# Output projections by Strassen's scheme, sums made ahead, and layer 1's values projected token by token

## The chip, the core and the metric

The kernel runs on one core of a Trainium2 chip. The metric is the device time of one execution in microseconds (us). Names of engines: PE is TensorE's matmuls, PEld its weight loads, DVE is VectorE, ACT is ScalarE, POOL is GpSimd, SP is SyncE, whose queue issues nearly all DMAs here.

## What is computed

Two layers over 1024 tokens of width 1024, all in float32. A layer normalises x, projects it, runs several groups of attention heads, multiplies their outputs with a gate, and projects the result y (1536 columns) back to 1024 columns, which are added to x:

```python
# layer 0                                   # layer 1
ya = global_gqa(qa, ka, va)                 yc = neighborhood_attn(qc, kc, vc, rpb_c[o])
yb = window_gqa(qb, kb, vb, sink, bias)     ym = memory_attn(qm, mk, mv)
ym = memory_attn(qm, mk, mv)                y = concatenate([yc, ym]) * silu(gate)
y = concatenate([ya, yb, ym]) * silu(gate)  x = x + y @ w_out_odd[o]
x = x + y @ w_out_even[e]                   return rmsnorm(x, final_norm_gain)
```

The product `y @ w_out` (1024 x 1536 times 1536 x 1024) is the output projection, once in each layer. Layer 1's neighbourhood attention has 16 heads of 64, which the kernel takes in 8 pairs, each with its own queries, keys and values projected from the normalised x.

## The kernel before

Everything is held transposed: 128 channels on the partitions, tokens along the row. Each float32 matrix is split into two parts, h (rounded) and l (the rest), and a product is three matmuls: h·h, h·l and l·h. So a projection of 128 channels over 512 tokens from 1024 inputs is 8 x 3 = 24 matmuls of 128x512. A weight unit is 4 blocks of 128x128: one DMA to `wraw` (`wload`, L100), then `wparts` (L112) makes `wh` and `wl` (L120 on POOL; L121 on DVE in layer 0 and on POOL in layer 1). There are four buffers of each.

The stages are: "prep" (memory keys, first projections), "l0" (four global head pairs with four memory heads between, then four window pairs), the output projection of layer 0, "l1" (four memory heads, then eight neighbourhood pairs, `near_head` L855), and the output projection of layer 1. A head's chain goes over all engines: scores on PE, row maximum on DVE, exponential on ACT, reciprocal on DVE, scaling on POOL (L815, L905), transposes on PE (`flip`, L96), split of the transposed tile on ACT and DVE (`p_parts`, L357), and the product with v on PE. Projections of the next heads stand between these steps on PE (`tokens`, L145, matmuls at L192), so that PE has work while a chain runs on. The order on each engine is not written by hand: the framework's list scheduler sets it when the kernel is built, from priorities (`AHEAD`, `ahead`) and its own idea of durations. Each engine then keeps to its order, and waits for semaphores.

The gated output of a head pair goes to DRAM (`gated`, L340, into `yd`) and is read back by the output projection (`y_parts`, L916). In layer 1 each pair's v is projected channel by channel (`v_pair`, L305) and then turned to tokens on the partitions by four transposes for each half (`v_sink`, L310, flips at L98).

`out_project` (L933) runs over two halves of 512 tokens, in each over 8 blocks of 128 output channels, and for each block over 12 blocks of y: 8 x 12 x 3 = 288 matmuls of 128x512 for a half, 576 for a layer (L136; the last block of all in two quarters of 256 tokens, L1001). After a block it adds x (L956), squares the sum (L957) and adds up the squares (L967); `done` then makes the norm of the half from them.

## Time and profile before

| | |
|---|---|
| median of 3 runs | 1590.55 us (1590.38 to 1591.15) |
| the profiled execution | 1589.67 us, of it 1587.5 us from the first to the last instruction (the span) |
| PE busy | 1541.1 us, 97% of the span, 8392 matmuls |
| DVE, ACT, POOL busy | 60%, 45%, 39% of the span |
| mean granted TensorE clock | 0.988 of full speed |
| moved by DMA | 167.46 MB, 105 GB/s over the span |

A busy share is an average over stages that differ. Matmuls are pipelined: one that lasts 0.4 us follows the one before it after less, so PE's pace is read from the starts. Idle time counts where something waits for the engine.

### The profile page before, as it was taken

The page shows a single profiled execution, that of the slowest core. Times are in us where ns is not written, and L with a number is a line of the kernel's source. Part 1 is how long each engine was busy: PE and PEld are TensorE (multiplying, and loading weights), DVE is VectorE, ACT ScalarE, POOL GpSimd, SP SyncE. Part 2 cuts the span into 40 slices and gives each one's busy share as a digit, 9 for nine tenths or more (in the row PEclk, how much of TensorE's full clock was granted, in tenths as well). Part 3 has the DMA queues.
Part 4 walks back from the last instruction along what each step waited for, and adds up shares of the span by engine and source line. Part 5 has one row for each costly group of instructions (what it writes and reads, how often), then busy time and mean ns, then how long its engine had stood idle before and what let it go on. Part 6 is the DMA issues. An engine that isn't in the chain of part 4 may idle for free.

```text
span 1587.5 us, 24171 instructions
## 1 busy us (share of the span) xinstructions
PE 1541.1 (97%) x8392; PEld 1322.0 (83%) x8392; DVE 952.8 (60%) x2123; ACT 707.1 (45%) x1626; POOL 626.7 (39%) x753
## 2 busy tenths in 40 slices
PE   6999999999999999989999999999999999999997
PEld 5899888988888788868778888888888888887886
DVE  7768677768776668855743444555556555554122
ACT  7644565566655445632213343444544444543110
POOL 2522324323322223325453344433433443445884
PEclk7999999999999999999999999999999999999998
DMA  9535211021101211146452232213223222235672
GB/s 352 178 100 160 83 34 55 20 87 47 60 14 54 89 41 57 57 147 209 153 177 81 87 112 88 77 69 102 73 73 102 71 75 89 83 108 186 228 261 80
DMA packets 96633, 167.46 MB, mean 105 GB/s; under 512 B 9472, under 2 KB 28160, under 8 KB 96512
## 3 DMA queue, kind: packets, MB, share of 16 engines
q1 hardware_dynamic: 95648, 165.19, 31.6%
q8 instruction: 66, 1.08, 0.3%
q10 hardware_dynamic: 864, 0.74, 0.2%
q14 instruction: 55, 0.45, 0.1%
HBM read 121.85 MB, written 34.60 MB: 99 GB/s over the span
## 4 chain that ended last, share of the span: by engine, by line
PE 89%; DVE 4%; DMA 3%; ACT 2%; issue 1%; POOL 0%; DVEq 0%; SPq 0%; ACTq 0%; POOLq 0%
PE pj L192 42%; PE tr L98 8%; PE sa L136 8%; PE pj L136 6%; PE pv L838 4%; PE s L136 3%; PE pj L637 3%; PE pv L874 2%; PE sa L807 2%; PE sa L808 2%; PE s L891 1%; PE s L892 1%; PE pv L535 1%; DMA wraw<-w_mem 1%; PE pj L390 1%
## 5 line engine op out<-in xcount | busy, mean ns | idle before, releaser
L192 PE MATMUL pj<-H,wh 128*128 128x512 f32 x1952 | 634.5, 402 | 2.2 <-ACT bt L957 1.5
L192 PEld LDWEIGHTS pj<-H,wh 128*128 128x128 f32 x1952 | 351.2, 188 | 64.8 <-POOL wh L120 1.9
L192 PE MATMUL pj<-H,wl 128*128 128x512 f32 x976 | 386.3, 396 | 0.0
L120 POOL TENSOR_SCALAR wh<-wraw 128x512 fp32r<-128x512 f32 x226 | 151.2, 671 | 433.4 <-PE pj L192 281.8
L90 ACT ACTIVATE ph<-tr 128x512 fp32r<-128x512 f32 (+2 forms) x336 | 178.4, 540 | 218.3 <-PE tr L98 204.9
L363 DVE TENSOR_TENSOR pl<-tr,ph 128x512 fp32r<-128x512 f32 (+2 forms) x336 | 205.2, 616 | 81.8 <-ACT ph L90 78.3
L192 PEld LDWEIGHTS pj<-H,wl 128*128 128x128 f32 x976 | 183.6, 188 | 38.1
L121 POOL TENSOR_TENSOR wl<-wraw,wh 128x512 fp32r<-128x512 f32 x136 | 178.9, 1321 | 24.6 <-ACT wh L90 14.5
L815 POOL TENSOR_SCALAR P<-P,st 128x1024 f32<-128x1024 f32 x64 | 80.3, 1256 | 128.2 <-DVE st L814 126.9
L905 POOL TENSOR_SCALAR pn<-pn,st 128x384 f32<-128x384 f32 (+1 forms) x128 | 71.2, 564 | 145.0 <-DVE st L904 144.0
L121 DVE TENSOR_TENSOR wl<-wraw,wh 128x512 fp32r<-128x512 f32 x116 | 91.7, 801 | 59.7 <-POOL wh L120 45.3
L98 PE MATMUL tr<-ident,P 128*128 128x128 f32 x816 | 122.5, 273 | 0.6 <-DVE pl L363 0.6
L98 PEld LDWEIGHTS tr<-ident,P 128*128 128x128 f32 x816 | 96.4, 140 | 9.8 <-DVE pl L363 2.3
L903 ACT ACTIVATE pn<-pn,st 128x384 f32<-128x384 f32 (+1 forms) x128 | 74.4, 582 | 46.7 <-DVE st L902 45.8
L813 ACT ACTIVATE P<-sa,st 128x1024 f32<-128x1024 f32 x64 | 71.5, 1117 | 40.4 <-PE tr L98 19.8
L812 DVE TENSOR_REDUCE st<-sa 128x1 f32<-128x1024 f32 x64 | 77.5, 1216 | 8.2 <-PE sa L808 8.1
L267 DVE TENSOR_TENSOR vt<-pj,rows 128x512 f32<-128x512 f32 x60 | 41.4, 689 | 67.5 <-PE pj L192 67.5
L899 DVE CUSTOM_DVE_ANT_0 pn<-s,bm 128x384 f32<-128x384 f32 x96 | 51.3, 554 | 44.6 <-PE s L892 40.8
L637 PE MATMUL pj<-ah,H 128*128 128x256 f32 x384 | 72.5, 285 | 0.0
L90 ACT ACTIVATE bt<-pv 64x512 f32<-64x512 f32 (+1 forms) x80 | 40.8, 510 | 60.5 <-PE pv L874 24.7
L838 PE MATMUL pv<-ph,va 128*128 128x256 f32 x256 | 66.7, 285 | 0.0
L838 PE MATMUL pv<-pl,va 128*128 128x256 f32 x256 | 65.4, 281 | 0.0
(324 smaller groups left out, 3096.4 us busy)
## 6 DMA issues: line engine op xcount, KB each, us to landing
wraw<-w_o SPq DMA_DIRECT2D x80, 256.0 KB, 2.6
wraw<-w_oe SPq DMA_DIRECT2D x48, 256.0 KB, 2.8
wraw<-w_oo SPq DMA_DIRECT2D x48, 256.0 KB, 2.9
wraw<-w_e SPq DMA_DIRECT2D x44, 256.0 KB, 2.6
k<-k SPq DMA_DIRECT2D x36, 256.0 KB, 3.7
wraw<-w_mem SPq DMA_DIRECT2D x32, 256.0 KB, 4.0
y<-yb SPq DMA_DIRECT2D x12, 512.0 KB, 2.6
y<-sg SPq DMA_DIRECT2D x24, 256.0 KB, 2.4
```

Source lines behind the costliest of these rows:

```text
L90: return self.nc.scalar.activation(out, in_, AF.Copy, scale=scale)
L98: self.turned = self.fence = self.nc.tensor.transpose(o, i, self.ident)
L120: nc.gpsimd.tensor_scalar(hf, raw, 1.0, 1.0, op0=OP.mult, op1=OP.mult)
L121: (nc.gpsimd if self.wsplit[1] == "pool" else nc.vector).tensor_tensor(lf, raw, hf, op=OP.subtract)
L136: self.last = nc.tensor.matmul(a[:, :n], s[:, k, :], moving(u * UNIT + k, c, n)[m], start=(u == units[0] and k == 0 and i == 0), stop=(u = ...
L192: last = nc.tensor.matmul(a[:, :n], s[:, kt % UNIT, :], m, start=(kt == 0 and i == 0), stop=(kt == KT - 1 and i == 2))
L363: nc.vector.tensor_tensor(pl[:, :n], tr[:, :n], ph[:, :n], op=OP.subtract)
L637: self.last = nc.tensor.matmul(a[:, b * 256:(b + 1) * 256], x[kt][:, t], w, start=(kt + b + i == 0), stop=(kt == KT - 1 and i == 2), skip_ ...
L812: nc.vector.tensor_reduce(st[:, 0:1], s, axis=AX.X, op=OP.max, negate=True)
L815: nc.gpsimd.tensor_scalar(pt, pt, st[:, 2:3], 0.5, op0=OP.mult, op1=OP.mult)
L838: nc.tensor.matmul(o[:, :256], v[:, c + k, kv, :], part[:, k * 256:(k + 1) * 256], start=(c + k == 0 and part is parts[0]), stop=(c + k == ...
L903: nc.scalar.activation(o, o, AF.Exp, bias=st[:, 1:2], accum_out=st[:, 2:3])
```

## The change

Both output projections are computed by Strassen's scheme in Winograd's form. The 1024 output channels, the 1536 y channels and the 1024 tokens are each cut in two, and the product of two 2x2 block matrices is made by 7 block products in place of 8. A block product is 4 blocks of 128 channels x 6 blocks of y x 3 matmuls of 128x512. The four sums of weight blocks (`weight_sums`) are made on POOL during layer 0's global heads and on DVE during layer 1's `values`, in pieces of 128x192, and go to DRAM (`sd`). The sums of y are made by POOL when a head's output is gated (`gated`) and go to DRAM in `yd`; the pairs are paired by `ROWS`, so that six head outputs come first and the other six each read their partner's sums back. `y_parts` loads one block of y for each product and splits it on ACT and DVE. The products' results are added into x on DVE as they come (`plus`). Weights of the output projections now come in units of 3 blocks, split on ACT and, in turn, DVE and POOL (`w_parts`).

Layer 1's values are no longer made pair by pair: `values` makes four pairs' v at once, with tokens on the partitions straight away (x as the stationary operand), in 8 blocks of 128 tokens x 24 matmuls, twice, between the memory heads; v goes to DRAM (`vd`), and each neighbourhood pair loads its own. In "l0" the l part of every weight unit moves from DVE to POOL.

```diff
-            with self.phase("l0", ("pool", "dve"), ...
+            with self.phase("l0", ("pool", "pool"), ...

+    def values(self, w, vd, g, side):
...
+        for b in range(8):
+            next(side, None)
+            p = self.ps("pj")
+            t = slice(b * 128, b * 128 + 128)
+            for kt, (h, l) in enumerate(ws):
+                for i, (x, m) in enumerate(((self.h[0], h), (self.h[0], l), (self.h[1], h))):
+                    nc.tensor.matmul(p, x[kt][:, t], m, start=(kt + i == 0), stop=(kt == KT - 1 and i == 2))
...
     def gated(self, sg, y, dst, other=None):
+            nc.vector.tensor_tensor(y, y, sg, op=OP.mult)
+            if other is None:
+                nc.gpsimd.tensor_tensor(sg[:, first], y[:, first], y[:, second], op=OP.subtract)
...
+            else:
+                nc.sync.dma_start(dst[:, 0:2, :], two(y))
+                nc.sync.dma_start(two(sg), other[:, 0:2, :])
+                nc.gpsimd.tensor_tensor(sg[:, second], y[:, first], sg[:, second], op=OP.subtract)
+                nc.gpsimd.tensor_tensor(sg[:, first], y[:, first], sg[:, first], op=OP.subtract)
+                nc.sync.dma_start(dst[:, 2:4, :], two(sg))
+                nc.gpsimd.tensor_tensor(y[:, second], sg[:, second], y[:, second], op=OP.subtract)
+                nc.sync.dma_start(dst[:, 4, :], y[:, second])
...
+        def sums():                                   # in weight_sums, 16 units of 4 sums
+            engine.tensor_tensor(a22, a22, a21, op=OP.add)
+            engine.tensor_tensor(a21, a11, a21, op=OP.subtract)
+            engine.tensor_tensor(a11, a22, a11, op=OP.subtract)
+            engine.tensor_tensor(a12, a12, a11, op=OP.subtract)
...
+        def product(y, bank, ws, start, cols=slice(0, 512)):
+            for u, (h, l) in enumerate(ws):
+                for k in range(3):
+                    for e, (s, m) in enumerate(((h, 0), (h, 1), (l, 0))):
+                        last = nc.tensor.matmul(bank, s[:, k, :], y[3 * u + k][m][:, cols], ...
...
+        for i in range(4):
+            product(first, xb[i], weights(i, "a11"), True)
...
+            product(y, yb[i], weights(i, "s1"), True)
+            product(y, xb[i], weights(i, "s2"), False)
+            product(y, xb[i], weights(i, "s3"), False)
+            product(y, yb[i], weights(i, "s4"), False)
...
+                end = product(y, xb[i], parts, True)          # a12
+            product(y, xb[i], weights(i, "a22"), True)
```

In layer 0's global heads the sums stand between the scalings of the softmax on POOL. Before, for the first head pair (P are the softmax tiles, st their statistics):

```order
L815 TENSOR_SCALAR P_2328<-P_2328,st_2327 128x1024
L120 TENSOR_SCALAR wh_2867<-wraw_2865 128x512
L815 TENSOR_SCALAR P_2375<-P_2375,st_2374 128x1024
L815 TENSOR_SCALAR P_2418<-P_2418,st_2417 128x1024
L815 TENSOR_SCALAR P_2469<-P_2469,st_2468 128x1024
```

And the same stretch of POOL now:

```order
L870 TENSOR_SCALAR P_2343<-P_2343,st_2342 128x1024
L1025 TENSOR_TENSOR bias_2289<-bias_2289 128x192
L129 TENSOR_SCALAR wh_2909<-wraw_2907 128x512
L870 TENSOR_SCALAR P_2396<-P_2396,st_2395 128x1024
L1026 TENSOR_TENSOR bias_2289<-bias_2289 128x192
L130 TENSOR_TENSOR wl_2910<-wraw_2907,wh_2909 128x512
L1027 TENSOR_TENSOR bias_2289<-bias_2289 128x192
L870 TENSOR_SCALAR P_2439<-P_2439,st_2438 128x1024
L1028 TENSOR_TENSOR bias_2289<-bias_2289 128x192
L870 TENSOR_SCALAR P_2493<-P_2493,st_2492 128x1024
```

Four sums and the l part of a weight unit came in; at most two added instructions stand in front of a scaling.

At the end of layer 0's last window pair, PE before (L535 is the product with v, L136 the output projection, k, q tiles of y, sa and pv banks of PSUM):

```order
L535 MATMUL pv_7715<-ph_7763,v_6090 128x2x128
L535 MATMUL pv_7715<-pl_7764,v_6090 128x2x128
L535 MATMUL pv_7715<-ph_7774,v_6090 128x2x128
L535 MATMUL pv_7715<-pl_7775,v_6090 128x2x128
L136 MATMUL sa_7915<-k_7875,wh_7991 128x512 x2
L136 MATMUL sa_7915<-k_7875,wl_7992 128x512
```

And PE now (L590 is the product with v, L1082 `product`):

```order
L1082 MATMUL tr_8087<-k_8230,wh_8267 128x512 x2
L1082 MATMUL tr_8087<-k_8230,wl_8268 128x512
L590 MATMUL pv_7925<-pl_7974,v_6278 128x2x128
L590 MATMUL pv_7925<-ph_7984,v_6278 128x2x128
L590 MATMUL pv_7925<-pl_7985,v_6278 128x2x128
L1082 MATMUL sa_8085<-q_8227,wh_8316 128x512 x2
L1082 MATMUL sa_8085<-q_8227,wl_8317 128x512
```

Here q_8227 and k_8230 hold sums of y that don't need the last pair. The first matmul that needs the last pair's y comes after 99 others of 128x512 (at the end of layer 1, after 93).

At the end of the program DVE made the first quarter's output (tr_16491) before the second quarter's norm (rq_v_16554 to iq_y_16556):

```order
L1118 SCALAR_TENSOR_TENSOR bm_16216<-bm_16216,gain_65,tr_16491 128x256 x2
L239 TENSOR_SCALAR rq_v_16554<-pv_16549 128x2
L1118 SCALAR_TENSOR_TENSOR yb_16339<-yb_16339,gain_65,tr_16491 128x256 x2
L1118 SCALAR_TENSOR_TENSOR yb_16408<-yb_16408,gain_65,tr_16491 128x256 x2
L571 RECIPROCAL iq_y_16556<-iq_t_16557 128x2
L572 TENSOR_TENSOR iq_t_16557<-iq_y_16556 128x2
L573 SCALAR_TENSOR_TENSOR iq_t_16557<-iq_t_16557,rq_v_16554 128x2
L574 SCALAR_TENSOR_TENSOR iq_y_16556<-iq_t_16557,iq_y_16556 128x2
L1118 SCALAR_TENSOR_TENSOR bm_16216<-bm_16216,gain_65,tr_16563 128x256 x2
```

Now both norms come first, and both outputs after them:

```order
L626 RECIPROCAL iq_y_16933<-iq_t_16934 128x2
L628 SCALAR_TENSOR_TENSOR iq_t_16880<-iq_t_16880,rq_v_16877 128x2
L627 TENSOR_TENSOR iq_t_16934<-iq_y_16933 128x2
L629 SCALAR_TENSOR_TENSOR iq_y_16879<-iq_t_16880,iq_y_16879 128x2
L628 SCALAR_TENSOR_TENSOR iq_t_16934<-iq_t_16934,rq_v_16931 128x2
L629 SCALAR_TENSOR_TENSOR iq_y_16933<-iq_t_16934,iq_y_16933 128x2
L1303 SCALAR_TENSOR_TENSOR H_15748<-H_15748,gain_65,tr_16886 128x256 x2
L1303 SCALAR_TENSOR_TENSOR yb_15753<-yb_15753,gain_65,tr_16886 128x256 x2
L1303 SCALAR_TENSOR_TENSOR yb_15754<-yb_15754,gain_65,tr_16886 128x256 x2
L1303 SCALAR_TENSOR_TENSOR H_15748<-H_15748,gain_65,tr_16940 128x256 x2
```

All twelve output instructions now stand behind the last norm.

## Rows read from the trace of the kernel before

**Rows 1.** The chain that ended last: shares of the span by engine.

```profile
PE 89%; DVE 4%; DMA 3%; ACT 2%; issue 1%; POOL 0%; DVEq 0%; SPq 0%; ACTq 0%; POOLq 0%
```

**Rows 2.** Stages: window, length, busy PE, PEld, DVE, ACT, POOL (counts), clock, DMA share, GB/s.

```profile
172.00:500.00 328.00, 328.00 (x2002) 288.30 (x2001) 240.78 (x388) 196.28 (x391) 107.49 (x114) 1.00 0.13 45
...
690.00:840.00 150.00, 142.10 (x627) 114.19 (x626) 87.06 (x125) 35.87 (x58) 66.00 (x66) 0.99 0.55 180
...
1122.00:1183.00 61.00, 60.58 (x317) 51.72 (x316) 35.01 (x104) 28.04 (x68) 24.38 (x32) 1.00 0.26 80
...
1421.00:1588.00 167.00, 153.06 (x763) 128.35 (x761) 46.94 (x123) 31.69 (x70) 115.64 (x127) 0.97 0.55 183
```

**Rows 3.** The chain in order of time: start, length, a piece of one kind.

```profile
1524.61 16.48 PE s L136 x72
```

**Rows 4.** Timeline of PE in a neighbourhood pair: start, length, instructions.

```profile
1144.32 0.60 PE L98 MATMUL pj<-ident,vt 128*128 128x128 f32 x4
1144.67 0.71 PE L192 MATMUL pj<-H,wh 128*128 128x512 f32 x2
1145.23 0.39 PE L192 MATMUL pj<-H,wl 128*128 128x512 f32 x1
1145.46 0.62 PE L192 MATMUL pj<-H,wh 128*128 128x512 f32 x2
1145.92 0.39 PE L192 MATMUL pj<-H,wl 128*128 128x512 f32 x1
```

**Rows 5.** PE's waits in 690 to 840: total us, times, longest.

```profile
PE sa L136 <- ACT k L90: 3.0, 1, 3.0
PE pj L192 <- ACT bt L957: 1.5, 1, 1.5
...
PE sa L136 <- ACT q L90: 0.8, 1, 0.8
```

**Rows 6.** PE's waits in 1421 to 1588.

```profile
PE tr L98 <- DVE iq_y L574: 3.8, 2, 3.2
PE pj L136 <- DMA mk<-y: 3.0, 1, 3.0
```

**Rows 7.** Timeline after layer 0's last product with v.

```profile
694.60 0.59 ACT L90 ACTIVATE bt<-pv 64x512 f32<-64x512 f32 x1 [1.59 <-PE pv L535]
...
696.10 1.22 DVE L345 TENSOR_TENSOR yb<-yb,sg 128x1024 f32<-128x1024 f32 x1
```

**Rows 8.** DMA issues: tiles, count, KB each, median us from issue to landing.

```profile
y<-yb SPq DMA_DIRECT2D x12, 512.0 KB, 2.6
...
q<-y SPq DMA_DIRECT2D x8, 512.0 KB, 7.5
...
q<-qa SPq DMA_DIRECT2D x6, 512.0 KB, 3.5
```

**Rows 9.** Groups of instructions: count, busy us, mean ns, idle before.

```profile
L121 POOL TENSOR_TENSOR wl<-wraw,wh 128x512 fp32r<-128x512 f32 x136 | 178.9, 1321 | 24.6 <-ACT wh L90 14.5 <-DVE e L604 3.0 <-PE pj L192 0.3
```

**Rows 10.** DVE's L121 in 172 to 500: ns minimum, median, maximum of one.

```profile
L121 DVE TENSOR_TENSOR wl<-wraw,wh x22: 672/691/1600, 186.7 to 487.6; 128x512 fp32r<-128x512 f32 x22
```

**Rows 11.** Groups of one neighbourhood chain, as in rows 9.

```profile
L903 ACT ACTIVATE pn<-pn,st 128x384 f32<-128x384 f32 x96 | 58.4, 609 | 43.7 <-DVE st L902 43.0 <-issue 0.3
L905 POOL TENSOR_SCALAR pn<-pn,st 128x384 f32<-128x384 f32 x96 | 56.4, 592 | 111.1 <-DVE st L904 110.2
...
L899 DVE CUSTOM_DVE_ANT_0 pn<-s,bm 128x384 f32<-128x384 f32 x96 | 51.3, 554 | 44.6 <-PE s L892 40.8 <-PE tr L98 3.1 <-PE s L891 0.3
```

**Rows 12.** Timeline of the end: DVE.

```profile
1577.70 0.15 DVE L239 TENSOR_SCALAR rq_v<-pv 128x2 f32<-128x2 f32 x1
1577.77 1.65 DVE L1118 SCALAR_TENSOR_TENSOR yb<-yb,gain,tr 128x256 f32<-128x256 f32 x4
1579.33 0.16 DVE L571 RECIPROCAL iq_y<-iq_t 128x2 f32<-128x2 f32 x1
```

**Rows 13.** The same view: the second quarter's output.

```profile
1581.34 0.87 DVE L1118 SCALAR_TENSOR_TENSOR bm<-bm,gain,tr 128x256 f32<-128x256 f32 x2 [1.26 <-ACT vt L90]
1582.13 1.65 DVE L1118 SCALAR_TENSOR_TENSOR yb<-yb,gain,tr 128x256 f32<-128x256 f32 x4
```

More of the change, by code (lines that the diff above doesn't have):

```diff
@@ L288, in k_pair @@
         nc = self.nc
-        kh = [self.st("k", [128, T], F32R) for _ in range(2)]
-        kl = [self.st("k", [128, T], F32R) for _ in range(2)]
+        kh, kl = zip(*[[self.st("k", [128, T], F32R) for _ in range(2)] for _ in range(2)])
         def sink(p, c, n):
@@ L338, in gate, with gated, gated_rows @@
         return sg
[L340 removed]
+    def gated(self, sg, y, dst, other=None):
         nc = self.nc
[L343 to L355 removed]
+        first, second = slice(0, 512), slice(512, T)
+        two = lambda t: t.rearrange("p (a n) -> p a n", a=2)
+        with self.ahead("gate"):
+            nc.vector.tensor_tensor(y, y, sg, op=OP.mult)
+            if other is None:
+                nc.gpsimd.tensor_tensor(sg[:, first], y[:, first], y[:, second], op=OP.subtract)
+                h, l = sg.bitcast(F32R)[:, second], y.bitcast(F32R)[:, second]
+                self.copy(h, y[:, second])
+                nc.vector.tensor_tensor(l, y[:, second], h, op=OP.subtract)
+                nc.sync.dma_start(dst[:, 0:4:2, :], two(y))
+                nc.sync.dma_start(dst[:, 1:4:2, :], two(sg))
+            else:
+                nc.sync.dma_start(dst[:, 0:2, :], two(y))
[5 more added lines that the diff above has]
+                nc.sync.dma_start(dst[:, 4, :], y[:, second])
+    def gated_rows(self, sg, nt, y, yd):
+        k = ROWS.index(nt)
+        self.gated(sg, y, yd[k], yd[k - 6] if k >= 6 else None)
     def p_parts(self, tr, n):
@@ L794, in load, with global_pair @@
         return t
[L796 removed]
+    def global_pair(self, qs, ks, v, kv, y, side):
         nc = self.nc
@@ L824, in global_pair @@
                 p = [pts[i, g, b] for b in range(2)]
+                with self.tc.issue_after(self.normal.ins):
+                    next(side, None)
                 o = self.ps("pv")
@@ new lines, in y_parts @@
+    def y_parts(self, yd, tags, kind):
+        nc = self.nc
+        parts = []
+        for k, t in enumerate(self.halves(tags, F32R)):
+            hi, lo = t[:, 0, :], t[:, 1, :]
+            raw = lo.bitcast(F32)
+            y1, y2 = yd[k], yd[6 + k]
+            with self.ahead("y"):
+                if kind == "y11":
+                    nc.sync.dma_start(t.bitcast(F32), y1[:, 2:4, :])
+                    parts.append((lo, hi))
+                    continue
+                src = dict(t1=y1[:, 1, :], t2=y2[:, 3, :], t3=y2[:, 2, :], y22=y2[:, 0, :], y21=y2[:, 1, :], t4=y2[:, 4, :])
+                nc.sync.dma_start(raw, src[kind])
+                self.split(hi, lo, raw)
+                parts.append((hi, lo))
@@ new lines, in weight_sums, with w_parts @@
+        units = [(i, u) for i in range(4) for u in range(4)]
+        if tag == "bias":
+            for unit in units:
+                load(*unit)
+                yield
+                sums()
+                yield
+        else:
+            for unit in units:
+                load(*unit)
+                if len(ready) > 2:
+                    sums()
+                    yield
+            while ready:
+                sums()
+                yield
+    def w_parts(self, raw, engine):
+        h, l = (self.st(t, [128, UNIT, 128], F32R, pool=self.base, bufs=4)[:, :3] for t in ("wh", "wl"))
+        hf, lf = (t.rearrange("p a b -> p (a b)") for t in (h, l))
+        self.copy(hf, raw)
+        engine.tensor_tensor(lf, raw, hf, op=OP.subtract)
+        return h, l
```

332 lines of the change are left out of this document (204 added, 128 removed).

## The prediction

> **What bounds the kernel now.** I read the chain that ended last first. It is PE for 89% of the span [rows 1]. An average over stages can hide another limit, so the table by stages comes next [rows 2]: in 172 to 500 us PE is busy for all of 328.00 us, in a neighbourhood pair for 60.58 of 61.00, in the two output projections for 142.10 of 150 and 153.06 of 167. DVE, the next one, has 35.01 of the pair's 61. So the time is the sum of what PE issues, plus few waits, most of them around the output projections. PE's pace is read where it runs without a break: 72 matmuls of 128x512 in 16.48 us [rows 3], which is 0.229 us each. The 0.4 us that one lasts is latency.
>
> **What goes from PE.** Before, an output projection is 8 x 12 x 3 x 2 = 576 matmuls of 128x512 (the last ones cut into quarters), now 7 x 4 x 6 x 3 = 504. Both layers together lose 144, at 0.229 us 33.0 us. Layer 1's values keep their number: 8 pairs x 48 before, 2 x 8 x 24 now, 384 both times. They lose their turning: 16 groups of four transposes. One group holds PE from 1144.32 to 1144.67, and the two matmuls behind it take 0.56 us where two others take 0.46 [rows 4]. So a group costs 0.35 + 0.10 = 0.45 us, and 16 of them 7.2 us. Together 40.2 us. PE gets nothing new: the sums of weights and of y are on POOL and DVE.
>
> **Does the work that moves find cover?** Three places.
>
> *Layer 0's global heads.* POOL is busy for 107.49 of 328.00 us there [rows 2]. It gets the l parts of 22 weight units [rows 10] at 1.32 us [rows 9], 29 us; 12 subtractions of y, 16 us; and 64 weight sums of 128x192. No row has that size: by length it is 0.50 us, by the whole 512-column row 1.32. I take 0.6, nearer to the first because the work grows with the columns: 38 us (32 to 85). That makes 190 us (up to 237) of 328, under PE. What queues behind a sum is a head's scaling (L870). In the new order at most two added instructions stand in front of one, 0.6 + 1.3 us, while PE has between a head's scores and their transposes some 20 us of other instructions, and 8 us at the least. I charge nothing; without that cover it would be 64 x 1.9 / 2 = 61 us at most.
>
> *The neighbourhood pairs.* A pair loses 48 matmuls (11.0 us) and two groups of transposes (0.9 us), and this was PE's filler behind the softmax chains: 61 us become 49. DVE has 35.01 us there now and loses four 128x512 steps of the values, ACT 28.04, POOL 24.38 plus up to three subtractions of 1.32 minus one weight unit of 2. All stay near 60% of 49. A chain's own steps are 0.55 + 0.61 + 0.59 us [rows 11] and some small ones, 3 to 4 us. Priced with the rates above, the new order of PE has typically 9 us of instructions between a block's scores and their transposes (9.5 before), 6 in the middle of the loop at the least. I charge nothing here for the typical pair.
>
> *The values themselves* are 88 us of unbroken matmuls between the memory heads. Their weights are split ahead of them, while two memory queries (22 us) are projected.
>
> **The seams.** Layer 0's projection waited 3.0 and 0.8 us for y of the last pair, layer 1's 3.0 us for y from DRAM and 3.8 us in two pieces for a norm, of which the longest, 3.2, is the end of the program [rows 5, 6]. Now the sums that don't need the last pair come first. After the last product with v PE has 99 matmuls in layer 0, 22.7 us, and 93 in layer 1, 21.3 us, before it needs that pair. The pair's new way is longer: 2.7 us to the end of the gating [rows 7], a load of the partner's sums, 3.5 us, two subtractions, 2.6, a write, 2.6, a read, 3.5 again, and the split, 0.6 as for the ACT row: 15.5 us [rows 7, 8, 9]. With both loads at 7.5 us, as the projection's busiest loads have it [rows 8], it is 23.5, and 1 to 2 us would show. I take the waits as gone: 3.0 + 0.8 + 3.0 + 0.6 = 7.4 us. The 1.5 us on ACT at the start of layer 1 I leave.
>
> *The end.* Before, the first quarter's output ran on DVE beside the second quarter's matmuls and in the gaps of its norm. Now all of it stands behind the last norm. That adds 0.87 + 1.65 = 2.5 us [rows 13] to the end. It takes away the 1.2 us or so by which those steps held up the second norm [rows 12], and adds five small steps at 0.2: +2.3 us (0 to 3.5).
>
> **New waits.** Some 230 more DMAs go through SP's one queue, where an issue that waits holds up the weights behind it, and the schedule was made from estimates. The rows give bounds: nothing, as in 172 to 500, or about 12 us, what both projections waited before [rows 5, 6]. I take 3 us, near the lower end, because PE's queue has the same depth of work between producers and users as before.
>
> **Sum.** The profiled execution took 1589.67 us: 1589.67 - 40.2 - 7.4 + 2.3 + 3 = 1547.4. The median of the runs shown lay 0.9 above it, so I forecast 1548 us, 2.7% less. Its own range is 1538 to 1557: no new waits, no longer end and the pairs' short waits gone below, all 12 us above.
>
> **One rule against the change.** A DVE subtraction with both inputs in SBUF takes 691 ns at the median and up to 1600 in layer 0 [rows 10], so something holds it up for 0.9 us at times. The Trainium skill (SBUF — State Buffer, "Who interferes with whom") says that a DVE instruction with two SBUF inputs and a GpSimd instruction that reads SBUF shut each other out for a whole instruction. The trace agrees with its number for single instructions; that the median stays at 691 says that few are hit. By the rule at its worst the forecast becomes the third rival below, 1568 us.
>
> **Rivals.**
> - *Feeding becomes the bound in the projections* (0.11). A weight unit now feeds 9 matmuls, not 12, so four buffers reach 8.2 us ahead, not 11.0. With a load at 7.5 us [rows 8], the h part on ACT at 0.5 and the l part on POOL at 0.75 x 1.32 = 1.0 [rows 9] a unit needs 9.0 us: 0.8 us short for each four units, 0.2 x 112 units = 22 us, 1570 us. Against it: the DMA engines are busy for 0.55 of these stages [rows 2], and with the same bytes in 13% less time for some 0.63.
> - *Slower: the softmax chain sets the pace of the neighbourhood pairs* (0.04). Its place is POOL's queue: in six pairs three subtractions of y, 4.0 us, and near them a weight unit of 1.9 us can stand in front of a scaling. A chain of 3.5 us then needs 9.4, against 9 us of cover, less where the order has 6. If every block is held so, a pair takes its 61 us again, and 8 x 11.9 = 95 us are lost: 1643 us, for the values' matmuls still have to be paid in their new place. It decides from 42 / 8 = 5.3 us a pair on. Against it: POOL is only half busy, and the scheduler put the scalings in front where it could.
> - *DVE and POOL shut each other out* (0.05). A projection has on DVE some 14 weight splits and 36 splits of y with two SBUF inputs. Were each held up by a whole POOL split of 1.0 us, 50 us would join DVE's own 66 us (0.52 and 0.69 us for these, 0.69 for 32 sums, 12 us for the norm and the next layer's input), and 116 us is what PE needs (504 x 0.229 = 115). PE would then wait for y now and then; half of what is over at single places, 10 us a layer, gives 1568 us.
> - That the change does less than it says isn't likely: the order on PE has 144 matmuls of 512 columns less and 64 transposes less. Below 1538 us I leave 0.03.
>
> **How the numbers follow.** The forecast has 0.77. The range of 1538 to 1562 takes it and the smaller part of the first and third rival, about 0.81. Within 0.2% of the old time, about what a measurement of this kernel can tell from no change, lies only a partial form of the second rival, 0.02; slower is its full form, 0.04; so faster has 0.94.
>
> **What would show it.** Right: some 8140 matmuls, PE still over 97% busy from 172 us to the last projection, a neighbourhood pair of 49 to 50 us, projections of some 115 us of matmuls each without a wait of 3 us at their start, and an end that is about 2 us longer. Wrong: PE waiting for `wh`, `wl` or a load of y inside the projections (first rival), transposes waiting for L962's scaling and pairs over 52 us (second), or DVE's two-input steps at a median well over 0.69 us with PE waiting for them (third).

## The result, and the profile after

The changed kernel takes 1564.36 us (median of 4 runs, 1561.52 to 1565.25) where the one before took 1590.47 on the same chip: ratio 0.9834 (95% interval 0.9817 to 0.9851). Timed again later it gave 1564.52 us, ratio 0.9837 (0.9823 to 0.9850). So it is 1.6% faster, 26 us, where 1548 us and 2.7% were forecast: 16 us are missing. The profiled execution took 1565.01 us, its span is 1563.2 us.

| | before | after |
|---|---|---|
| PE busy, matmuls | 1541.1 us, 8392 | 1510.8 us, 8166 |
| DVE, ACT, POOL busy | 60%, 45%, 39% | 65%, 50%, 45% |
| moved by DMA | 167.46 MB | 228.33 MB |
| start of PE's last matmul | 1580.5 us | 1553.6 us |

First the chain that ended last, by engine; it answers to [rows 1]:

```profile
PE 80%; DMA 8%; DVE 5%; ACT 2%; issue 2%; POOL 1%; SPq 1%; DVEq 0%; ACTq 0%; POOLq 0%
```

DMA holds 8% where it held 3%, PE 80% where it held 89%. Next the table by stage, answering to [rows 2], columns as there: the global heads, a neighbourhood pair, the first seam with the hand-over to layer 1, and most of layer 1's projection.

```profile
172.00:500.00 328.00, 328.00 (x2004) 288.85 (x2002) 237.78 (x371) 198.85 (x396) 179.73 (x208) 1.00 0.29 97
1122.00:1171.00 49.00, 49.00 (x264) 42.10 (x263) 30.90 (x99) 25.59 (x64) 23.14 (x30) 1.00 0.33 100
690.00:840.00 150.00, 141.64 (x630) 114.22 (x628) 100.87 (x157) 70.13 (x127) 70.04 (x57) 0.98 0.64 211
1432.00:1545.00 113.00, 110.68 (x503) 90.13 (x502) 67.10 (x103) 53.76 (x99) 54.09 (x49) 1.00 0.54 181
```

The global heads stay full of PE, with POOL at 179.73 us. Those 49 us of the pairs are all PE. The first seam, where layer 0's last head pair meets its output projection, is no better filled than before (141.64 of 150; 142.10 before).

To say where the time went I add up **lost time** over each stretch: from each matmul's start to the next one's, what exceeds its own share of an unbroken run (0.229 us for 512 columns, 0.174 for 384, 0.115 for 256, 0.057 for a transpose). It holds waits and a slow clock alike. A seam reaches from 15 us before the projection's first matmul to 20 us after the last pair's last product with v. The last four columns are experiments below.

| lost time, us | before | change | no split | no sums | neither | t1 stored in layer 1 |
|---|---|---|---|---|---|---|
| up to the first seam | 92.6 | 92.9 | 92.9 | 93.2 | 91.4 | 92.0 |
| first seam | 13.3 | 18.3 | 12.5 | 18.3 | 15.6 | 13.5 |
| from there to 1000 us | 13.2 | 17.5 | 20.4 | 16.8 | 14.2 | 21.3 |
| near pairs | 27.6 | 24.4 | 24.4 | 23.3 | 23.6 | 23.9 |
| second seam | 6.6 | 10.0 | 4.9 | 9.5 | 5.1 | 5.1 |
| the rest | 7.4 | 7.4 | 4.7 | 6.5 | 5.1 | 7.0 |
| sum | 160.7 | 170.4 | 159.9 | 167.7 | 155.0 | 162.9 |
| of the span from the first seam on, at half clock | 3.4 | 17.1 | 6.8 | 17.1 | 10.2 | 6.8 |

What PE issues fell by 36.6 us at that pace (1418.5 to 1381.9). With the 3.6 us by which transposes cost more than their pace, 40.2 were forecast. But lost time rose by 9.7 us, at the two seams and behind the first one. The near pairs' fall of 3.2 matches those transposes.

Two timelines show how the first seam is lost: ACT's queue, then the matmul of PE that waits for it. In brackets: the idle time before the instruction, and what ended it.

```profile
693.05 1.09 ACT L99 ACTIVATE ph<-tr 128x512 fp32r<-128x512 f32 x2
697.62 0.63 ACT L99 ACTIVATE H<-H 128x512 fp32r<-128x512 f32 x1 [3.48 <-DMA H<-y]
698.16 1.07 ACT L99 ACTIVATE ph<-tr 128x512 fp32r<-128x512 f32 x2
```

```profile
698.79 0.38 PE L590 MATMUL pv<-ph,v 128*128 128x256 f32 x1 [2.13 <-ACT ph L99]
```

The split of a block of y (H, for the third set of products) waits 3.48 us for its transfer. Behind it in ACT's queue stand two copies that the last window pair needs, and PE waits 2.13 us for them. At the second seam transfers hold ACT for only 1.2 us, but ACT is full. Its groups from 1405 to 1436 us, with count, busy us, mean ns, and the idle time before them:

```profile
L99 ACT ACTIVATE ph<-tr 128x384 fp32r<-128x384 f32 x10 | 4.7, 486 | 2.3 <-PE tr L107 2.3
L99 ACT ACTIVATE H<-H 128x512 fp32r<-128x512 f32 x5 | 3.0, 626 | 0.8 <-DMA H<-y 0.8
...
L99 ACT ACTIVATE k<-k 128x512 fp32r<-128x512 f32 x4 | 2.5, 625 | 0.4 <-DMA k<-y 0.4
...
L99 ACT ACTIVATE q<-q 128x512 fp32r<-128x512 f32 x2 | 1.2, 622 | 0.0
```

Eleven splits of y (H, k, q) stand among ten of the last pair's copies, and from 1422 to 1432 us ACT is busy for 9.93 us of 10, DVE for all 10.00. The waits of PE that are named there are short; the first is for the sum of the pair's output on DVE, which stood behind a split's subtraction of 1.09 us in its queue:

```profile
PE pv L931 <- DVE yb L940: 1.3, 1, 1.3
PE pv L931 <- ACT ph L99: 0.4, 1, 0.4
```

Of this seam's 10.0 us another 3.9 are lost at half clock behind them. In the kernel before, layer 1 stored y in two parts and had no splits there. And the granted clock falls behind each such stretch; the same columns as above:

```profile
692.00:700.00 8.00, 4.29 (x31) 3.45 (x31) 4.12 (x8) 3.28 (x6) 1.14 (x2) 1.00 0.74 236
700.43:707.25 6.82, 6.15 (x20) 4.91 (x19) 1.85 (x4) 1.81 (x4) 0.00 (x0) 0.50 0.78 253
1419.00:1424.00 5.00, 3.51 (x20) 2.40 (x18) 5.00 (x17) 4.28 (x11) 4.52 (x4) 1.00 1.07 393
1424.05:1430.88 6.83, 6.68 (x19) 5.18 (x20) 6.83 (x20) 6.78 (x17) 3.22 (x4) 0.50 0.84 286
```

PE is busy for 4.29 of 8 us, then runs 6.82 us at 0.50, that is 1.2 GHz. The same at 1419 (3.51 of 5, then 6.83 us), and a third time for 3.4 us at 673. What the slow clock costs is read from the chain in order of time, by pieces of 18 matmuls (start, length):

```profile
673.17 5.95 PE pj L1082 x18
...
703.31 6.04 PE tr L1082 x18
...
1426.76 6.30 PE s L1082 x18
...
1434.42 4.13 PE pj L1082 x18
```

At full clock 18 take 4.13 us, in these three pieces about 2 us more each, 5.9 us together. All lost time inside the three slow stretches is 9.4 us, waits in them included; half of their 17.1 us, 8.5, is the most that a halved clock can cost. The kernel before had one such stretch, of 3.4 us, with 1.6 us lost. So some 4 to 7 of the missing 16 us are clock. A second profile of the same kernel, taken with the last experiments, lost 18.7 and 9.4 us at the seams, so the seams' loss comes again; its slow stretches lay in part elsewhere (20.5 us from the first seam on, in five pieces, only 3.4 us of them at the second seam).

### The profile page after: what moved, and what is told of

Read it like the earlier page. It is cut to its first block, busy times and chain, and to the rows that moved or that the text cites. A ratio compares the mean times of both kernels' runs of the same rounds, so it can differ in the third digit from the quotient of the medians.

```text
span 1563.2 us, 24589 instructions
## 1 busy us (share of the span) xinstructions
PE 1510.8 (97%) x8166; PEld 1292.1 (83%) x8166; DVE 1016.0 (65%) x2226; ACT 788.9 (50%) x1798; POOL 700.8 (45%) x795
## 2 busy tenths in 40 slices
DMA packets 156671, 228.33 MB, mean 146 GB/s; under 512 B 13184, under 2 KB 95360, under 8 KB 155520
## 3 DMA queue, kind: packets, MB, share of 16 engines
q8 instruction: 64, 1.05, 0.3%
## 4 chain that ended last, share of the span: by engine, by line
PE 80%; DMA 8%; DVE 5%; ACT 2%; issue 2%; POOL 1%; SPq 1%; DVEq 0%; ACTq 0%; POOLq 0%
PE pj L201 34%; PE tr L107 8%; PE pv L895 4%; PE pj L1082 3%; PE pj L353 3%; PE tr L1082 3%; PE sa L1082 3%; PE pv L931 3%; PE pj L692 2%; PE s L1082 2%; PE sa L862 2%; PE sa L863 2%; PE pv L1082 2%; PE pj L145 2%; DMA wraw<-w_o 1%
## 5 line engine op out<-in xcount | busy, mean ns | idle before, releaser
L201 PE MATMUL pj<-H,wh 128*128 128x512 f32 x1696 | 556.9, 403 | 1.4 <-DVE sg L377 0.7
L201 PEld LDWEIGHTS pj<-H,wh 128*128 128x128 f32 x1696 | 305.8, 189 | 54.4 <-DVE sg L377 1.0
L201 PE MATMUL pj<-H,wl 128*128 128x512 f32 x848 | 336.0, 396 | 0.0
L201 PEld LDWEIGHTS pj<-H,wl 128*128 128x128 f32 x848 | 159.6, 188 | 33.1
L129 POOL TENSOR_SCALAR wh<-wraw 128x512 fp32r<-128x512 f32 x114 | 74.7, 656 | 230.0 <-PE pj L201 199.3
L130 POOL TENSOR_TENSOR wl<-wraw,wh 128x512 fp32r<-128x512 f32 x114 | 153.3, 1347 | 22.9 <-ACT wh L99 13.9
L1053 POOL TENSOR_TENSOR wl<-wraw,wh 128x384 fp32r<-128x384 f32 x56 | 62.7, 1121 | 127.4 <-ACT wh L99 101.4
L99 ACT ACTIVATE wh<-wraw 128x384 fp32r<-128x384 f32 (+1 forms) x138 | 73.4, 540 | 84.2 <-PE tr L1082 16.6
L508 POOL TENSOR_SCALAR P<-P,st 128x256 f32<-128x256 f32 x64 | 32.1, 517 | 125.6 <-DVE st L506 125.3
L353 PE MATMUL pj<-k,H 128*128 128x512 f32 x256 | 81.8, 392 | 4.4 <-DVE ph L364 2.0
L956 DVE CUSTOM_DVE_ANT_0 pn<-s,bm 128x384 f32<-128x384 f32 x96 | 52.1, 553 | 26.4 <-PE tr L107 13.3
```

The source lines that it names most:

```text
L99: return self.nc.scalar.activation(out, in_, AF.Copy, scale=scale)
L130: (nc.gpsimd if self.wsplit[1] == "pool" else nc.vector).tensor_tensor(lf, raw, hf, op=OP.subtract)
L201: last = nc.tensor.matmul(a[:, :n], s[:, kt % UNIT, :], m, start=(kt == 0 and i == 0), stop=(kt == KT - 1 and i == 2))
L353: nc.tensor.matmul(p, x[kt][:, t], m, start=(kt + i == 0), stop=(kt == KT - 1 and i == 2))
```

## The experiments

Theory S (A in the first four) says that the seams hold the loss; the rivals put it into feeding the products, the values' stage, or elsewhere. Times are medians; "against the change" is the difference of the ratios from 0.9837, times 1590 us, uncertain by 3 us. The interval stands behind each ratio.

**Accumulator banks of layer 0.**

```diff
-x = [self.ps("pj"), sa[0][:, 0, :], sa[1][:, 0, :], tr[1]]
-y = [tr[0], self.ps("pv"), sa[0][:, 1, :], sa[1][:, 1, :]]
+x = [self.ps("pj"), sa[0][:, 0, :], sa[1][:, 0, :], sa[0][:, 1, :]]
+y = [sa[1][:, 1, :], tr[0], self.ps("pv"), tr[1]]
```

> Edit: layer 0's output projection takes its eight accumulator banks in another order, so that the first five products use the banks of pj and of the scores, and those of the transposes and of pv come last. Theory A (most of what is missing is lost where the last head pair of a layer meets the products, because TensorE runs out of work that may start, and the granted clock falls to half behind it): between 692 and 707.3 us of the changed kernel's profile TensorE waited 0.84 + 0.27 + 2.13 + 0.46 + 0.67 = 4.4 us, and the stretch at half clock behind it, 700.4 to 707.3, held 3.9 us of lost time. With the fourth product, 18 matmuls of 0.229 = 4.1 us, free to start before those waits, they should shrink and the fall of the clock with them: 1556 to 1561 us (3 to 8 below the change). Rival B (the loss is in feeding the products, their weights' splits and the sums on VectorE and GpSimd): within 1.5 us of the change, 1563 to 1566. Rival C (the fourth product's weights or y are late as well): no more than 1 us.

Measured: 1574.36 us, 0.9899 (0.9884 to 0.9913), 10 us slower. Theory A in this form fell. ACT again:

```profile
696.86 0.63 ACT L99 ACTIVATE H<-H 128x512 fp32r<-128x512 f32 x1 [4.11 <-DMA H<-y]
...
700.27 0.63 ACT L99 ACTIVATE q<-q 128x512 fp32r<-128x512 f32 x1 [2.36 <-DMA q<-y]
```

The schedule now puts the split of H and four splits of a further set (q, k) ahead of the copies, and PE's wait for the copies grows from 2.8 to 5.1 us. I took from this that PE did not lack work, but waits for what stands behind the splits. That gave Theory S.

**The last gate of layer 1 in a tile of its own.**

```diff
-self.gated_rows(self.gate(w, O_G + j), j, y, yd)
+self.gated_rows(self.gate(w, O_G + j, "mk" if j == 7 else "sg"), j, y, yd)
...
```

> Edit: in layer 1 the gate of the last head pair is written to the tile of the memory keys, which is free by then, and no longer to the one gate tile, which the Strassen sums of the pair before still hold. Theory A': the gate's read of its pj bank came only at 1428.3 to 1430.8 us because the gate tile was held until the sums of the pair before had been written out, so the second product had no bank; the stretch 1421 to 1431 us lost 7.0 us, 3.9 of them at half clock, where the kernel before lost 0.6. With a tile of its own: 1557 to 1561 us (4 to 7 below the change), and no stretch at half clock near 1424. Rival B (feeding of the products): the wait moves to weights or y, within 1.5 us of the change.

Measured: 1566.94 us, 0.9852 (0.9837 to 0.9867), no gain. The second seam lost 13.9 us, and the copies were waited for there too (2.3 us). The held bank wasn't the cause.

**One set of splits later (layer 0).**

```diff
-self.split(hi, lo, raw)
+with self.tc.issue_after(after.ins) if after else nullcontext():   # t2: the last pair's last copy
+    self.split(hi, lo, raw)
```

> Edit: in layer 0 the splits of the third set of y (the H tiles) are queued on ScalarE behind the last pair's last copy of transposed scores. Theory A'': the split at 697.62 us waited 3.48 us for its transfer at the head of ScalarE's queue, and the two copies behind it held TensorE 2.13 us; with the split behind them that wait goes, and with it some of the 3.9 us at half clock: 1558 to 1562.5 us (2 to 6 below the change). Rival (the copies were held by the order of the transposes, or the same y is needed soon after): within 1.5 us of the change.

Measured: 1561.94 us, 0.9817 (0.9804 to 0.9829), 3 us better, at the edge of what can be told. The first seam lost 16.4 us instead of 18.3: splits of the second set, which stood ahead of the pair's copies before too, now waited for their transfers there:

```profile
686.81 0.63 ACT L99 ACTIVATE q<-q 128x512 fp32r<-128x512 f32 x1 [1.82 <-DMA q<-y]
...
689.36 0.63 ACT L99 ACTIVATE k<-k 128x512 fp32r<-128x512 f32 x1 [1.51 <-DMA k<-y]
```

**Layer 1's values by pair again.**

```diff
-v = self.load("v", vd[j // 2][j % 2], (128, 8, 256)).rearrange("p b (h d) -> p b h d", h=2)
+v = self.v_pair(w, O_V + j)
-if h in (0, 2):
-    self.values(w[O_V:], vd, h // 2, side)
+for _ in range(4):
+    next(side, None)
```

> Edit: layer 1's values go back to one projection and its transposes for each head pair, as in the kernel before; all else is the change's. The change's own edit took 16 groups of 4 transposes x 0.45 = 7.2 us from TensorE here, but its stage (740 to 980 us of the changed profile) lost 17.0 us where the kernel before lost 11.9 in the same work. Theory A (the loss lies at the seams, the values gave what was forecast): 7.2 above the change, 1570 to 1573 us. Rival V (the values' stage gave most of its gain back in waits): 1 to 3 above the change, 1565 to 1567.5.

Measured: 1589.66 us, 0.9987 (0.9975 to 0.9998), 24 us slower, far over both forecasts. Its lost time: 28.1 us between the first seam and 1000 us (17.5 in the change), 10.2 us of that stretch at half clock, and 15.4 at the second seam. PE waits there from 820 to 980 us:

```profile
PE s L486 <- DMA mk<-kv: 4.1, 2, 2.6
PE pj L201 <- DVE q L103: 2.7, 2, 2.5
PE pv L520 <- DVE pl L418: 1.8, 1, 1.8
```

I read this so: the values' 88 us of matmuls are what the memory heads' chains and the sums hide behind; without them the stage waits and the clock falls. But the edit also places the sums in bunches of four, so how much of the 24 us is the values' own is not shown.

**No splits.** This is the test of Theory S.

```diff
+if kind in ("t1", "t2"):
+    parts.append((lo, lo))
+    continue
 self.split(hi, lo, raw)
```

> Leaves out: the splits into high and low part of the second and third set of y (t1 and t2) in both layers; the products read the loaded tile for both parts, so TensorE's work and the transfers stay, and 24 splits, each one copy on ScalarE and one subtraction on VectorE, go. Theory S (after the first runs: what is missing at the seams is these splits in the in-order queues of ScalarE and VectorE, in front of the last head pair's own copies, exponentials and closes): the loss that the change shows over the kernel before at the two seams, 5.5 us (640 to 740 us) and 6.9 us (1410 to 1431 us), goes: 1550 to 1556 us. Rival W (the products wait for the transfer of y or of the weights, split or not): 1561 to 1566 us. Rival C (only the work of TensorE in the last pair is too thin, so the clock falls whatever the splits do): 1558 to 1564 us, with half clock at the same places.

Measured: 1554.43 us, 0.9763 (0.9744 to 0.9782), 12 us better. The table shows it at the seams: 12.5 and 4.9 us. The stretches of the change's fall, in this run:

```profile
700.43:707.25 6.82, 5.55 (x27) 4.34 (x25) 3.53 (x5) 3.63 (x7) 1.00 (x1) 1.00 0.74 270
1419.00:1424.00 5.00, 4.28 (x23) 3.26 (x22) 3.99 (x17) 4.30 (x12) 3.73 (x7) 1.00 1.05 397
1424.05:1430.88 6.83, 6.83 (x36) 5.76 (x35) 4.11 (x7) 3.56 (x8) 2.07 (x3) 1.00 0.68 226
```

The clock stays at 1.00 at both seams. Transfers and PE's work are the same (DMA share 1.05 at 1419 us), so neither the loads (rival W) nor thin work alone (rival C) hold it. What PE still waits for at the first seam is the sum of the pair's output and, later, parts of weights:

```profile
PE pv L590 <- DVE yb L600: 1.9, 2, 1.5
PE sa L1085 <- ACT wh L99: 1.3, 1, 1.3
PE sa L1085 <- DVE wl L1056: 1.1, 1, 1.1
```

**Both sets late, in both layers.** The edit of one set late, for t1 and t2.

> Edit: in both layers all splits of the second and third set of y are queued on ScalarE behind the last pair's last copy of transposed scores. Theory S, order alone (a split whose y is late must not stand in front of the copies): the waits of the last pair for ScalarE's copies go (2.8 us and the half clock behind them in layer 0, the bunch of 1420 to 1427 us in layer 1), and 12 splits of 0.53 us, 6.4 us, follow the pair, of which the fourth product covers 4.1 in layer 0: 1555 to 1561 us. Rival S2 (it is the splits' number, not their place: behind the pair they hold the next products just as long): 1562 to 1569 us.

Measured: 1562.48 us, 0.9813 (0.9796 to 0.9831), 4 us better. By the ratio that is 1561 us, the upper end of Theory S's forecast; by the median it is the lower end of rival S2's: the run doesn't decide between them. The profiled execution, one of 1564.8 us, lost 17.4 us at the first seam and 9.2 at the second. In layer 0 the wait moves behind the pair, where a product of t1 now waits for its split (v), and another for a weight's part:

```profile
PE tr L1083 <- ACT v L99: 1.8, 1, 1.8
...
PE sa L1083 <- ACT wh L99: 1.6, 1, 1.6
```

In layer 1 no split stands ahead of a copy any more, and still the clock falls, for 3.4 us. PE waits there for a scaling on POOL, in front of which POOL makes three sums of y in 3.8 us:

```profile
PE tr L107 <- POOL pn L962: 1.4, 1, 1.4
```

So it isn't enough to put the splits behind the copies.

**No sums of weights.**

```diff
-side = self.weight_sums(self.io["w_oe"], sd, "bias", nc.gpsimd)
+side = iter(())
...
-side = self.weight_sums(self.io["w_oo"], sd, "pn", nc.vector)
+side = iter(())
```

> Leaves out: the sums of the weights in both layers with their loads and stores; the products read unsummed weights in their place. Rival V (part of what is missing lies in the memory stage of layer 1, where VectorE makes 64 of these sums between 780 and 980 us and the changed kernel lost 5.1 us more than the kernel before): 1558 to 1561 us. Rival D (GpSimd's sums in layer 0's global pairs, 1.1 us of the stretch's loss, and the transfers slow everything a little): 1554 to 1560 us. Theory S (the seams alone): within 1.5 us of the change, 1563 to 1566 us.

Measured: 1562.68 us, 0.9818 (0.9803 to 0.9833), 3 us better, at the edge of what can be told. What PE waited for from 840 to 900 us, in the change and in this run:

```profile
PE pj L353 <- DVE ph L364: 2.0, 1, 2.0
PE tr L107 <- DVE rq_y L223: 1.3, 1, 1.3
PE pj L353 <- DVE ph L360: 1.2, 1, 1.2
PE pj L353 <- DVE q L103: 1.0, 1, 1.0
```

```profile
PE tr L107 <- DVE rq_y L223: 1.6, 1, 1.6
```

The values' three waits, 4.2 us, come from DVE's queue with the sums in it, and go with them. The whole stretch from the first seam to 1000 us lost only 0.7 us less, with a fall of the clock at 796.7 us, 3.4 us long; the unedited change has that fall too in its second profile (796.2 us), so it isn't the edit's.

**Neither splits nor sums.** Both edits.

> Leaves out: both the splits of the second and third set of y and the sums of the weights in both layers. If the forecast missed for these two reasons, side work at the seams (11 us by the run without splits) and VectorE's sums in front of the values (2 to 5 us by the run without sums), the two together give what the forecast said, 1548 us: 1547 to 1552 us. If something else in the change holds the time too, 1553 us or more.

Measured: 1549.3 us, 0.9747 (0.9734 to 0.9760). Against 1590.5 that is 1550 us (1548.2 to 1552.3); the forecast was 1548. So the time that is missing goes with these two kinds of side work, but for some 2 us. That the sum comes out is in part luck: the seams still lose 20.7 us here, 0.8 more than before, where the forecast had 7.4 less, and smaller losses elsewhere make up for most of that.

**Splits on POOL.** `nc.gpsimd` for both steps of t1's and t2's splits.

> Edit: the splits of the second and third set of y, both halves of them, are made on GpSimd, which stood idle from 693 to 707 us and for 1.4 to 3.9 us at a time between 1405 and 1436 us. Theory S: ScalarE and VectorE keep their queues for the last pair; a split costs GpSimd some 2.3 us (1.0 + 1.3), 12 of them 27 us in a layer, most of it under the products of y11: 1553 to 1560 us. Rival G (GpSimd is late with them, the products of t1 wait): 1564 to 1575 us.

Measured: 1578.80 us, 0.9921 (0.9906 to 0.9937), 13 us slower, more than rival G said, and not in its way: no product of t1 waits for POOL. At the first seam PE waits for the last pair's own scaling, which now stands behind the splits in POOL's queue:

```profile
PE tr L107 <- POOL P L575: 3.8, 1, 3.8
```

POOL's copy (L1002) and subtraction (L1003) of a split, and the kernel's own copy of a weight unit (L129), of the same shape:

```profile
L1002 POOL TENSOR_SCALAR H<-H 128x512 fp32r<-128x512 f32 x12 | 18.4, 1541 | 14.7 <-DMA H<-y 14.7
L1003 POOL TENSOR_TENSOR H<-H 128x512 fp32r<-128x512 f32 x12 | 17.5, 1458 | 0.1
L129 POOL TENSOR_SCALAR wh<-wraw 128x512 fp32r<-128x512 f32 x114 | 74.4, 653 | 229.7 <-PE pj L201 197.9 <-DMA wraw<-w_mem 15.6 <-DMA wraw<-w_e 7.5
```

A split takes 3.0 us, not the 2.3 expected. Most of the excess is its copy: 1.54 us, where 1.0 was taken and L129 needs 0.65. The edit writes the copy with one multiplication (`1.0, None`), L129 with two (`1.0, 1.0`); that the form makes the difference is likely, but no run has the split in L129's form. So the run speaks against this edit, and not against splits on POOL as such.

**t1 stored in two parts.** Splits made where the first six rows are gated, long before the seam; t2 late.

```diff
 nc.gpsimd.tensor_tensor(sg[:, first], y[:, first], y[:, second], op=OP.subtract)
+parts = [self.st(t, [128, 512], F32R) for t in self.t1_tags]   # ph, pl in layer 0; own tiles in layer 1
+self.split(*parts, sg[:, first])
+for i, t in enumerate(parts):
+    nc.sync.dma_start(dst[:, 4 + i, :], t.bitcast(F32))
```

> Edit: the second set of y (t1, differences of the first six rows of heads) is split when those rows are gated and stored in two parts, so the projection loads it ready; the third set (t2), which holds the last pair's rows, is split behind the last pair's last copy. Theory S: no split of y is left in front of the last pair's chain and none that the second four products wait for; the seams lose what they lost without splits (14.5 us from 640 to 740, 3 from 1410 to 1440 us, against 20.4 and 10), less some 0.5 us for the 12 earlier splits in busy pairs: 1553 to 1557 us, and no more than one fall of the clock at the seams. Rival S2 (the number of splits counts, wherever they stand): 1559 to 1565 us.

Measured: 1568.58 us, 0.9868 (0.9851 to 0.9885), 5 us slower. The seams did as expected (11.1 and 5.3 us lost, no fall of the clock), but before them 103.6 us were lost instead of 92.9. Layer 0's `ph` and `pl` have three buffers each, and a global pair waits at 446 us:

```profile
PE pv L900 <- DVE pl L423: 3.6, 1, 3.6
```

**With the banks of the first experiment.**

> Edit: that of t1 stored in two parts, and beside it the accumulator banks of layer 0 in the order of the first experiment. In the first experiment that order made things 10 us worse: the products that started sooner put y's splits further ahead of the copies in ScalarE's queue. Theory S: without splits there, the same order now helps or does nothing, 0 to 4 us below the version with t1 stored alone: 1550 to 1556 us. Rival (the bank order itself is bad, by taking the bank of transposes or scores from the last pair too early): some 10 us above the version with t1 stored alone.

Measured: 1580.92 us, 0.9941 (0.9926 to 0.9956), 12 us above the version without them. Of the two forecasts the rival's held: splits weren't all that made those banks bad: PE still waited 3.1 us for the pair's copies, 2.6 us at 745 us for a sum on DVE before it could use a bank again, and 5.6 us at 814 us for `wl` on DVE. Why DVE was late there I didn't settle.

**t1's parts in the weights' tiles, and the sums by near pairs.** `pool=self.base, bufs=4` with the tags `wh` and `wl`; then besides three `next(side, None)` behind each near head.

> Edit: as with t1 stored in two parts, but the two parts are made in tiles of the weights' two tags (four buffers each) and no longer in layer 0's ph and pl, which held up the global pairs by some 9.9 us of lost time (2.6 at 240 to 260, 1.8 at 320 to 340, 5.5 at 440 to 460 us). Theory S: the seams stay as the version with t1 stored had them (13.8 us lost at the first, some 4 at the second, without a fall of the clock) and the 9.9 us go: 1554 to 1560 us. Rival (the weights come late instead, at the 12 places where the split is made): 1562 to 1570 us.

> Edit: that of t1 through the weights' tiles, and beside it layer 1's sums of weights on VectorE are made in the near pairs, three steps behind each head, with a tile of their own, in place of the memory stage. Theory V: the waits of the values' products between 847 and 887 us go as they did without sums, and the near pairs, where VectorE is some two thirds busy, take 64 sums without being held: 2 to 5 us below the version through the weights' tiles. Rival: the sums delay the near pairs' chains: equal or up to 5 us above it.

Measured: 1615.90 us, 1.0168 (1.0154 to 1.0182), and 1632.92 us, 1.0279 (1.0261 to 1.0296). Both are far slower than either of their forecasts. As I read it, the parts hold weight buffers; PE waits for weights from 1000 to 1200 us:

```profile
PE pj L201 <- POOL wh L129: 9.9, 3, 4.6
```

34 us of the near pairs then ran at half clock. The second run's 17 us more lie mostly before the pairs (42.2 us lost from the first seam to 1000 us, 26.7 in the first). It says nothing clean about the sums.

**Sums of layer 1 on POOL.** `nc.gpsimd` for `nc.vector`.

> Edit: layer 1's sums of weights are made on GpSimd in place of VectorE, nothing else. Rival V (with the sums left out, the waits of the values' products between 847 and 887 us went, 4.7 us of lost time, so they come from VectorE's queue there): 2 to 5 us below the change, 1559 to 1562 us, with the values' waits gone. Theory S alone (this stage does not matter), or GpSimd's own chain of probabilities becoming late instead: within 1.5 us of the change, 1563 to 1566 us, or slower by up to 3.

Measured: 1572.49 us, 0.9887 (0.9872 to 0.9902), 8 us slower, more than any of the forecasts. The values' waits went, but there are three falls of the clock (13.7 us) around PE's waits for DVE, among them 4.2 us for rq_y at 838 us and 3.0 us for pl. The first of the three, at 796 us, is in the second profile of the unedited change too.

**t1 stored in layer 1 alone.** Layer 1 has room for two more tiles, layer 0 by my count hasn't. The splits of t2 are late in both layers.

> Edit: t1 is stored in two parts in layer 1 alone, in a pair of tiles that nothing else uses; layer 0 keeps its splits of t1; t2's splits stand behind the last pair's last copy in both layers. Theory S: layer 1's seam loses some 4 us instead of 10 without a fall of the clock, as where both layers stored t1; layer 0's loses 18 us as with late splits alone, and its global pairs nothing: 5 to 9 us below the change, 1555.5 to 1559.5 us. Rival S2 (the work comes back in the near pairs): 1561 to 1565 us.

> Edit: as the version with t1 stored in layer 1, and in layer 0 t1's splits too stand behind the last pair's last copy. Theory S: the last pair's copies wait for no transfer (1.0 us of waits for ScalarE's copies in place of 3.5), and the products of t1 wait for the splits instead (2 to 4 us after 704 us, as with both sets late): within 1.5 us of the version with t1 stored in layer 1. Rival: the half clock behind the pair goes and 2 to 4 us with it.

Measured: 1558.32 us, 0.9800 (0.9786 to 0.9813), and with t1 late in layer 0 1560.96 us, 0.9806 (0.9790 to 0.9821), no difference. The first was timed again beside the unedited change:

> The changed kernel itself, unedited, timed beside the version with t1 stored in layer 1 on the same chip, since the differences of 2 to 6 us on which the reading of the experiments rests are near what one set of runs can tell: 1562 to 1566 us, ratio 0.982 to 0.985. If it comes out at 1560 us or less, the gains read from late splits (2.5 us) and from storing t1 in layer 1 (6 us) shrink by as much.

> The version with t1 stored in two parts in layer 1, unedited, beside the change: 1557 to 1560 us, 4 to 8 us below the change if Theory S's gain is real; within 2 us of it if the first measurement was chance.

Measured: 1564.52 us, 0.9837 (0.9823 to 0.9850), and 1557.66 us, 0.9796 (0.9782 to 0.9809). The gain of 6 to 7 us came twice, with all work kept; this version beats both kernels. It holds both edits, t1 stored in layer 1 and t2 late. Its second seam, in the first of its two profiles:

```profile
1412.00:1443.00 31.00, 30.21 (x161) 25.44 (x160) 23.61 (x59) 21.74 (x50) 12.50 (x15) 1.00 0.88 320
```

So the number of splits in the program doesn't set the seam's loss. This seam loses 5.1 us when half of its splits are made earlier and the others late, 4.9 when all are left out, and 9.2 when all are only moved behind the pair's last copy. Each figure is of one profile.

## Why the forecast missed

- *What goes from PE* was right: 36.6 us at the unbroken pace and 3.2 of the 3.6 us of the transposes' excess.
- *Layer 0's global heads*: right. No loss up to the first seam (92.9 us; 92.6 before).
- *The neighbourhood pairs*: right. From the gating (L390) at 1163.0 us to the one at 1407.6 us lie five pairs, 48.9 us each on average.
- *The end*: right. From PE's last matmul to the end 9.6 us; 7.0 before: +2.6, forecast +2.3.
- **The step that failed is the seams: "I take the waits as gone", -7.4 us.** They lost 8.4 us more than before (5.0 + 3.4), so this term is off by 15.8. The reckoning of the last pair's own y held: no product waited for it, and the waits of 3.0, 0.8 and 3.0 us that were named are gone. Others came in their place. The reckoning counted matmuls after the last product with v, and the loss is before it, while the pair's own chain still runs. The splits of two sets of y stood in the text only as 0.6 us of a path and as a cause of contention. Their place in ACT's and DVE's queues, ahead of the copies that the last pair waits for, wasn't looked at, though the order on ACT shows it. The question of what is queued behind a waiting instruction was asked for POOL and left out for ACT and DVE. Without these splits the seams lose 17.4 us instead of 28.3, so 10.9 of the 15.8 us are theirs. The other 4.9 stay open: even then the seams lose only 2.5 us less than before, not 7.4, and PE still waits 2.4 us for parts of weights at the first. That the place in the queue is the cause is shown for the wait of 2.8 us in layer 0; for layer 1 it is shown that the splits are, and not which queue.
- *The clock* has no term. The trace of before had one fall, 3.4 us at 697 us, behind a wait at the same place (columns as in the table by stage):

```profile
694.20:697.10 2.90, 0.30 (x3) 0.09 (x1) 1.83 (x3) 0.99 (x2) 0.00 (x0) 1.00 0.74 246
697.10:700.50 3.40, 3.02 (x7) 2.19 (x8) 2.04 (x4) 1.50 (x3) 0.00 (x0) 0.50 0.85 278
```

  That more waits there could mean more of it might have been read from it. It makes some 4 to 7 of the 13.3 us (9.7 + 3.6) by which lost time stands above what the transposes leave. The Trainium skill (TensorE: Matmul & The Clock Gate, "HAM oscillation — how this bites in real kernels") describes a matmul loop that falls back to half rate at its waits for DMA again and again; the trace agrees in that the clock falls to 1.2 GHz three times behind waits, though the longest of them, 2.13 us, was for a copy on ACT and not for DMA.
- *New waits, +3 us*, held less than came: from the first seam to 1000 us 4.3 us more. Waits of the values, 4.2 us, go where DVE's sums are left out, though the stretch as a whole lost only 0.7 us less in that run. "Unbroken matmuls between the memory heads" overlooked that the sums share DVE with the values' own splits.
- The sum: 15.8 + 4.3 + 0.4 (other stretches) - 3 = 17.5, of 17.6 us between the forecast sum and the profiled execution.
- *Rivals.* Feeding: 5.4 us of waits for `wl` in the whole of both projections, not 22; not the bound. The softmax chain: no, the pairs take 48.9 us. DVE against POOL: in layer 0 the splits' subtractions of H and q keep a median of 0.69 us (640 to 860 us), so contention isn't what made these late. In layer 1 those of H and q do too (1397 to 1545 us), but the seven of k have a median of 0.91 us, up to 1.79; what held these wasn't tried, and in the change PE waits for no split's subtraction in the projections.

Left open: the first seam still loses 13 us in the best version that keeps all work, as before. Whether t1 can be stored in layer 0 without holding up its pairs wasn't tried beyond two tile pairs.

## What to carry to other kernels

Where a stage's preparation is scheduled into the end of the stage before, look at the in-order queue of each helper engine: what stands in front of the last chain's steps, and does it wait for a transfer? Move such work to where its inputs are long ready, into tiles nothing else needs; the two tiles borrowed here from the weights' ring cost some 50 us, more than the seams could give. Moving the work behind the last chain's steps was not enough here. Where TensorE gets thin, look at the granted clock behind it: here a fall cost some 2 us for each 18 matmuls of 512 columns.

## What the runs showed that was not expected

- A good part of the loss is clock: 17.1 us at 0.50 from the first seam on, which cost some 6 to 8.5 us. Before the three stretches PE was busy for 7.52 us of 9, 4.29 of 8 and 3.51 of 5, with no single wait over 2.13 us.
- The amount of work in an edit said little of its cost: the values by pair, 7.2 us of transposes, cost 24 us together with the other order of the sums, and two tiles taken from the weights' ring some 50 us.
- POOL took 1.54 us to copy 128x512 with one multiplication, but 0.65 with two (L129), in the same run; a subtraction took it 1.46. ACT's copy takes 0.63.
